# Two attention edits: GpSimd scales the probabilities; ScalarE and VectorE take turns at copying their transposes

## The chip, the cores and the metric

The kernel runs on one core of a Trainium2 chip. The metric is the device time of one execution in microseconds (us); the times are medians over executions. The engines are TensorE (PE, its weight loads PEld), VectorE (DVE), ScalarE (ACT), GpSimd (POOL) and SyncE (SP, which mostly issues transfers). Each engine works through its own instructions in program order.

## The reference

A trunk of two layers over 1024 tokens of width 1024, in f32. Layer 0 mixes with a state-space and a convolution branch and isn't touched by the change. Layer 1 mixes with two attentions, 8 heads each. Every layer ends with a normalised residual and a gated projection.

```python
def masked_softmax(s, mask):
    s = jnp.where(mask, s.astype(jnp.float32), NEG)
    m = jnp.max(s, axis=-1, keepdims=True)
    e = jnp.exp(s - m) * mask
    return e / jnp.maximum(jnp.sum(e, axis=-1, keepdims=True), 1e-30)
...
    # NSA: compressed, selected (top 8 blocks of 64 keys) and windowed (512 keys) attention
    o = g[:, :, 0] * o_cmp + g[:, :, 1] * o_sel + g[:, :, 2] * o_win
...
        # MLA: causal attention over all keys, 64 + 32 features a head
        s = jnp.einsum('bqhd,bkhd->bhqk', qb, k).astype(f32) * scale
        mask = kpos[None] <= (t0 + jnp.arange(Q_BLOCK))[:, None]
        return jnp.einsum('bhqk,bkhd->bqhd', masked_softmax(s, mask), v)
```

## The kernel before

A scheduler that simulates a timeline of the engines orders the instructions of the whole program: the code gives the work and its dependences, and the order on each engine follows from the durations that the scheduler assumes. So an edit that moves an instruction to another engine changes the order on all of them from there on.

**NSA** (`nsa`, about 970 to 1217 us of the profiled execution) takes 8 blocks of 128 queries in the order 1, 2, 0, 3, 4, 5, 6, 7. A block i is done in two halves of 4 heads (`gp`). A half begins with the compressed part (L1315) and then takes two branches: the window (`br=1`, at most 640 keys) and the selection (`br=0`, 128(i+1) keys). **MLA** (`mla`, about 1228 to 1425 us) takes 16 steps: twice the same 8 blocks, 4 heads each, all causal keys.

In both, the 4 heads of a half go through in *groups* of `hg` heads, so many that a group's scores fit one pair of banks: 4 heads up to 256 keys, 2 up to 512, else 1 (`group_size`). A group's way is:

- scores S on TensorE (L1333 and L1338 in NSA; L1518, L1521 and L1522 in MLA; masks L1263) into one of two score buffers in PSUM (`bank2`);
- `softmax_group`: the row maximum, negated, on VectorE (L1234); exp with row sums on ScalarE (L1237), from the score buffer into a probability buffer P in SBUF (which frees the score buffer); the reciprocal of the sum, with the branch's gate, on VectorE (L1241 to L1244); the scaling of P by it, one instruction a head, in place (L1246);
- `transpose_group`: TensorE transposes P in tiles of 128x128 (L1258) into banks of 512 columns, of which three rotate (`ps_t`), and each filled bank is copied to PT in SBUF (L1259). When all the transposes have read P, the buffer is free for another group's exp.

When a branch's four heads are transposed, a run of value matmuls (PV; L1353 in NSA, L1530 in MLA) adds PT times V into the output o, and `store_y` gates and stores it (L1273).

NSA has four probability buffers, MLA three:

```python
                        P = Ps[:, np_ % 4].rearrange("p (h n) -> p h n", h=hg)   # nsa
...
                P = self.t4(name="P").rearrange("p (h n) -> p h n", h=hg)        # mla, 3 buffers
```

GpSimd meanwhile copies gates for groups of 4 heads (L1345), issues the transfers of the query masks (L1295), holds back the load of MLA's rotary keys (L104, `qmslot`) until its place is free, and computes low parts of weights (L108).

Of the kernel before, what the change touches and what calls it, by code (L numbers as in the profile page):

```python
# [11 lines left out]
OP = mybir.AluOpType  # L12
# [10 lines left out]
class Trunk:  # L23
# [1205 lines left out]
    def softmax_group(self, S, n, ginv, P):  # L1229

        nc = self.nc
        hg = S.shape[1]
        nm = self.small.tile([128, 4], F32, tag="nm", name="nm", bufs=4)
        nc.vector.tensor_reduce(out=nm[:, 0:hg], in_=S[:, :, 0:n], op=OP.max, axis=AX.X, negate=True)  # L1234
        sm = self.small.tile([128, 4], F32, tag="sm", name="sm", bufs=4)
        for h in range(hg):
            nc.scalar.activation(out=P[:, h, 0:n], in_=S[:, h, 0:n], func=AF.Exp, bias=nm[:, h:h + 1],  # L1237
                                 accum_out=sm[:, h:h + 1])
        r = self.small.tile([128, 4], F32, tag="sr", name="sr", bufs=4)
        if ginv is None:  # L1240
            nc.vector.tensor_scalar(out=r[:, 0:hg], in0=sm[:, 0:hg], scalar1=1e-30, scalar2=None, op0=OP.max)  # L1241
        else:
            nc.vector.scalar_tensor_tensor(out=r[:, 0:hg], in0=sm[:, 0:hg], scalar=1e-30, in1=ginv, op0=OP.max, op1=OP.mult)
        nc.vector.reciprocal(r[:, 0:hg], r[:, 0:hg])  # L1244
        for h in range(hg):
            nc.vector.tensor_scalar(out=P[:, h, 0:n], in0=P[:, h, 0:n], scalar1=r[:, h:h + 1], scalar2=None, op0=OP.mult)  # L1246

    def transpose_group(self, P, hg, nk, PT, s0):

        nc = self.nc  # L1250
        kb = 4 // hg
        for k0 in range(0, nk, kb):
            n = min(kb, nk - k0)
            ps = self.bank()
            for k in range(n):
                for h in range(hg):
                    c = 128 * (k * hg + h)
                    nc.tensor.transpose(ps[:, c:c + 128], P[:, h, 128 * (k0 + k):128 * (k0 + k) + 128], self.ident)  # L1258
            nc.scalar.copy(PT[:, k0:k0 + n, s0:s0 + hg],  # L1259
                           ps[:, 0:128 * n * hg].rearrange("p (k h t) -> p k h t", h=hg, t=128))  # L1260

    def add_mask(self, S, mask):
        self.nc.tensor.matmul(S, self.ident_bf, mask, start=False, stop=False, skip_group_check=True)  # L1263
# [377 lines left out]
```

## Time and profile before

| | |
|---|---|
| median of 3 runs | 1639.42 us (1637.12 to 1641.62) |
| profiled execution | 1643.63 us, its span 1641.8 us |
| granted TensorE clock, mean | 0.955 of full speed |
| TensorE busy | 93% of the span |
| VectorE, ScalarE, GpSimd busy | 61%, 39%, 22% |

Busy shares are of the whole span, in which NSA and MLA are some 27%. A granted clock of 1.00 is TensorE's upper level, 2.4 GHz, and 0.50 its lower, 1.2 GHz. In the timeline and in grouped rows a matmul's duration overlaps the next one's start; in the chain the pieces adjoin.

### The profile page before, as it was taken

What the parts mean: (1) busy time and instruction counts of PE and PEld (TensorE: products, weight loads), DVE (VectorE), ACT (ScalarE), POOL (GpSimd) and SP (SyncE); (2) the same over time, 40 slices, a digit from 0 to 9 for tenths busy, and PEclk for the clock granted to TensorE, in tenths of its full rate; (3) what the DMA queues carried; (4) which work ended last, traced back from release to release, by engine and by line L of the source; (5) the groups of instructions that cost most, each with busy time, mean ns of one, the idle gap of its engine ahead of it and who ended that gap; (6) DMA issues with size and microseconds to landing.
All of it is one profiled execution on the core that took longest, in us unless ns stands there. A gap on an engine that the chain in (4) does not pass through costs nothing.

```text
span 1641.8 us, 22311 instructions
## 1 busy us (share of the span) xinstructions
PE 1522.7 (93%) x8284; PEld 1193.1 (73%) x8284; DVE 1004.4 (61%) x2248; ACT 636.3 (39%) x1297; POOL 360.4 (22%) x319
## 2 busy tenths in 40 slices
PE   4799899779998999799998979999999999999998
PEld 4697787667786888698876756666666676777787
DVE  6899999778435554751586246777744566444411
ACT  5332122166213333322342127777654565412210
POOL 4528633421225002312222200000000000132400
PEclk8899999889999999899999979999996999999999
DMA  8012453413424324242722264120043230422421
GB/s 244 14 52 79 139 180 111 146 52 129 157 78 142 128 87 135 82 143 85 180 90 90 77 193 125 54 67 22 27 98 85 66 92 25 143 95 94 151 87 68
DMA packets 140380, 168.65 MB, mean 103 GB/s; under 512 B 19432, under 2 KB 107232, under 8 KB 140272
## 3 DMA queue, kind: packets, MB, share of 16 engines
q1 hardware_dynamic: 135568, 155.82, 30.8%
q0 software_dynamic: 4544, 11.38, 2.3%
q8 instruction: 66, 1.08, 0.3%
q14 instruction: 42, 0.34, 0.1%
q10 hardware_dynamic: 160, 0.01, 0.0%
HBM read 112.10 MB, written 50.99 MB: 99 GB/s over the span
## 4 chain that ended last, share of the span: by engine, by line
PE 72%; DVE 17%; DMA 3%; ACT 2%; issue 2%; SPq 2%; POOL 1%; ACTq 0%; DVEq 0%; POOLq 0%
PE S L114 39%; PE tr L1258 7%; DVE conv L264 5%; PE o L1353 5%; PE tr L114 3%; PE o L1530 3%; PE S L1338 2%; PE S L1521 2%; PE S L1522 2%; PE S L1333 2%; PE S L1518 1%; PE tr L802 1%; PE S L1263 1%; SPq L1294 1%; PE tr L973 1%
## 5 line engine op out<-in xcount | busy, mean ns | idle before, releaser
L114 PE MATMUL S<-xT,wt 128*128 128x512 f32 x768 | 188.3, 401 | 4.3 <-DVE ext L249 4.3
L1234 DVE TENSOR_REDUCE nm<-S 128x1 f32<-128x640 f32 (+7 forms) x132 | 129.4, 981 | 101.8 <-PE S L1522 65.1
L114 PE MATMUL S<-X,wt 128*128 128x512 f32 x768 | 184.6, 396 | 5.8 <-ACT wt L107 2.3
L114 PE MATMUL S<-wo,Y 128*128 128x512 f32 x768 | 181.4, 395 | 5.0 <-DVE gb L688 3.6
L114 PE MATMUL S<-wg,hT 128*128 128x512 f32 x720 | 176.8, 403 | 9.5 <-ACT wg L107 4.0
L114 PEld LDWEIGHTS S<-xT,wt 128*128 128x128 f32 x768 | 144.9, 192 | 35.8 <-DVE ext L249 5.1
L114 PEld LDWEIGHTS S<-X,wt 128*128 128x128 f32 x768 | 143.1, 190 | 37.0 <-issue 4.0
L114 PEld LDWEIGHTS S<-wo,Y 128*128 128x128 f32 x768 | 143.8, 189 | 35.7 <-DVE gb L688 3.9
L114 PEld LDWEIGHTS S<-wg,hT 128*128 128x128 f32 x720 | 136.7, 193 | 42.2 <-ACT wg L107 7.3
L264 DVE SCALAR_TENSOR_TENSOR conv<-ext,conv 128x1024 f32<-128x1024 f32 x116 | 148.9, 1284 | 2.3
L108 POOL TENSOR_TENSOR wt<-raw,wt 128x1024 fp32r<-128x1024 f32 x34 | 82.8, 2451 | 115.9 <-ACT wt L107 115.8
L1237 ACT ACTIVATE pslot<-S,nm 128x640 f32<-128x640 f32 (+7 forms) x128 | 89.9, 709 | 25.6 <-DVE nm L1234 14.6
L1259 ACT COPY PT<-tr 128x512 f32<-128x512 f32 (+3 forms) x172 | 80.2, 492 | 46.5 <-PE tr L1258 42.3
L1258 PE MATMUL tr<-ident,pslot 128*128 128x128 f32 x528 | 84.7, 284 | 0.0
L1353 PE MATMUL o<-PT,vslot 128*64 128x256 f32 x528 | 84.5, 391 | 0.0
L1258 PEld LDWEIGHTS tr<-ident,pslot 128*128 128x128 f32 x528 | 58.7, 142 | 29.8 <-issue 20.8
L97 DVE TENSOR_SCALAR rs_v<-ss 128x1 f32<-128x1 f32 x32 | 4.9, 153 | 119.4 <-ACT lh L93 99.1
L1338 PE MATMUL S<-kst,qslot 112*128 112x512 f32 (+3 forms) x192 | 74.4, 400 | 0.0
L1333 PE MATMUL S<-kst,qslot 128*128 128x512 f32 (+3 forms) x192 | 70.3, 366 | 2.3 <-ACT pslot L1237 1.4
L787 POOL TENSOR_TENSOR lh<-lh 128x1024 f32<-128x1024 f32 x16 | 39.9, 2496 | 120.1 <-DVE lh L786 96.5
L852 DVE SCALAR_TENSOR_TENSOR ov<-ov,S 128x1024 f32<-128x1024 f32 (+1 forms) x17 | 19.7, 1157 | 73.3 <-issue 44.7
L93 ACT ACTIVATE lh<-S 128x1024 f32<-128x1024 f32 x16 | 16.4, 1028 | 123.3 <-issue 94.8
(433 smaller groups left out, 2858.8 us busy)
## 6 DMA issues: line engine op xcount, KB each, us to landing
h_dram<-lh POOLq DMA_DIRECT2D x16, 512.0 KB, 3.2
hr<-h_dram SPq DMA_DIRECT2D x14, 512.0 KB, 3.4
raw<-ev_w_in SPq DMA_DIRECT2D x16, 256.0 KB, 4.3
raw<-ev_w_in SPq DMA_DIRECT2D x8, 512.0 KB, 6.9
raw<-ev_w_out SPq DMA_DIRECT2D x8, 512.0 KB, 4.4
t<-ple_gate SPq DMA_DIRECT2D x8, 512.0 KB, 5.9
raw<-ple_gate SPq DMA_DIRECT2D x8, 512.0 KB, 6.3
lh<-x SPq DMA_DIRECT2D x8, 512.0 KB, 3.9
```

The costliest lines, as they stand in the source:

```text
L108: (eng or self.nc.gpsimd).tensor_tensor(lo, raw, hi, OP.subtract)
L114: self.nc.tensor.matmul(ps, l, r, start=n == 0, stop=n == len(seq) - 1)
L264: nc.vector.scalar_tensor_tensor(out=last if s == 30 else acc, in0=src, scalar=wc, in1=acc, op0=OP.mult, op1=OP.add)
L787: nc.gpsimd.tensor_tensor(hv, hv, xr, OP.add)
L1234: nc.vector.tensor_reduce(out=nm[:, 0:hg], in_=S[:, :, 0:n], op=OP.max, axis=AX.X, negate=True)
L1237: nc.scalar.activation(out=P[:, h, 0:n], in_=S[:, h, 0:n], func=AF.Exp, bias=nm[:, h:h + 1], accum_out=sm[:, h:h + 1])
L1258: nc.tensor.transpose(ps[:, c:c + 128], P[:, h, 128 * (k0 + k):128 * (k0 + k) + 128], self.ident)
L1259: nc.scalar.copy(PT[:, k0:k0 + n, s0:s0 + hg], ps[:, 0:128 * n * hg].rearrange("p (k h t) -> p k h t", h=hg, t=128))
L1333: nc.tensor.matmul(o_, QA[:, hd], KA[:, y, ks], start=True, stop=False)
L1338: nc.tensor.matmul(o_, qb[:, hd], KB[:, y, ks], start=False, stop=True)
L1353: nc.tensor.matmul(o[64 * y:64 * y + 64].rearrange("p g t -> p (g t)"), self.vsw[:, k0 + kt, 128 * br + 64 * y:128 * br + 64 * y + 64], PT ...
L1530: nc.tensor.matmul(o[64 * b:64 * b + 64, q], vm[:, kt, vs], PT[:, kt, 2 * b + q], start=(kt == 0), stop=(kt == nk - 1))
```

## The change

The scaling of P goes from VectorE to GpSimd (192 instructions: 128 in NSA, 64 in MLA). The copies of the transposes (258), all on ScalarE before, alternate between ScalarE and VectorE by the number of the bank and of the group.

```diff
         for h in range(hg):
-            nc.vector.tensor_scalar(out=P[:, h, 0:n], in0=P[:, h, 0:n], scalar1=r[:, h:h + 1], scalar2=None, op0=OP.mult)
+            nc.gpsimd.tensor_scalar(out=P[:, h, 0:n], in0=P[:, h, 0:n], scalar1=r[:, h:h + 1], scalar2=None, op0=OP.mult)
 
     def transpose_group(self, P, hg, nk, PT, s0):
...
                     nc.tensor.transpose(ps[:, c:c + 128], P[:, h, 128 * (k0 + k):128 * (k0 + k) + 128], self.ident)
-            nc.scalar.copy(PT[:, k0:k0 + n, s0:s0 + hg],
-                           ps[:, 0:128 * n * hg].rearrange("p (k h t) -> p k h t", h=hg, t=128))
+            copy = nc.vector.tensor_copy if (k0 // kb + s0 // hg) % 2 else nc.scalar.copy
+            copy(PT[:, k0:k0 + n, s0:s0 + hg], ps[:, 0:128 * n * hg].rearrange("p (k h t) -> p k h t", h=hg, t=128))
```

Since the scheduler orders anew, three places are shown in the order of the instructions. In the names, `pslot` is NSA's probability buffers, `tr` a transpose bank, `S` a score buffer, `o` the output, `PT` the transposed probabilities. NSA's groups are numbered in order of the program, 0 to 87; those of block 6 are 56 to 71.

First TensorE in the second half of block 6, from the transposes of group 62 (seven, of a selection head) on. Before, the value matmuls and the transposes of group 63 come next, and then the scores of group 66:

```order
L1258 MATMUL tr<-ident,pslot 128x128 x7
L1353 MATMUL o<-PT,vslot 64x256
L1258 MATMUL tr<-ident,pslot 128x128 x4
L1333 MATMUL S<-kst,qslot 128x512
L1263 LDWEIGHTS mbf
L1263 MATMUL S<-mbf 128x128
L1338 MATMUL S<-kst,qslot 128x512
```

In the changed kernel the same transposes, the first row, are followed at once by the scores of group 68 (selection, 896 keys, in two parts of 512 and 384), then by the transposes of group 63 and the scores of group 69:

```order
L1258 MATMUL tr<-ident,pslot 128x128 x7
L1333 MATMUL S<-kst,qslot 128x512
L1338 MATMUL S<-kst,qslot 128x512
L1333 MATMUL S<-kst,qslot 128x384
L1263 LDWEIGHTS mbf
L1263 MATMUL S<-mbf 128x128
L1338 MATMUL S<-kst,qslot 128x384
L1258 MATMUL tr<-ident,pslot 128x128 x7
L1333 MATMUL S<-kst,qslot 128x512
```

What moved: scores stand six groups ahead of the transposes instead of four.

Second ScalarE at the same place in the changed kernel: two exps of 640 keys (groups 64 and 65), two copies (of groups 61 and 62), the exps of groups 66 and 67, and so on:

```order
L1237 ACTIVATE pslot,sm<-S,nm 128x640 x2
L1260 COPY PT<-tr 128x3x128
L1260 COPY PT<-tr 128x4x128
L1237 ACTIVATE pslot,sm<-S,nm 128x640 x2
L1260 COPY PT<-tr 128x3x128
L1260 COPY PT<-tr 128x4x128
L107 CAST Y_9420<-yt 128x2x128
L1237 ACTIVATE pslot,sm<-S,nm 128x896
```

The exp of group 66 stands behind the copy of group 62; the other copies of these groups are on VectorE.

Third GpSimd at the end of NSA, where it had only the gating copies before; the difference shows the scalings that go in, and those of MLA behind the copy that holds back MLA's keys:

```order
 L104 COPY Y_9420<-Y_9420 128x1 x2
+L1246 TENSOR_SCALAR pslot<-pslot,sr 128x896 x4
+L1246 TENSOR_SCALAR pslot<-pslot,sr 128x640 x4
+L1246 TENSOR_SCALAR pslot<-pslot,sr 128x1024 x4
+L1246 TENSOR_SCALAR pslot<-pslot,sr 128x640 x4
+L1246 TENSOR_SCALAR pslot<-pslot,sr 128x1024 x4
 L104 COPY qmslot<-KAm 96x1
+L1246 TENSOR_SCALAR P<-P,sr 128x128 x4
```

GpSimd's own other work keeps its order, with scalings between.

## Rows read from the trace of the kernel before

**Rows 1.** The page: span, and busy time of each engine with its share.
```profile
span 1641.8 us, 22311 instructions
PE 1522.7 (93%) x8284; PEld 1193.1 (73%) x8284; DVE 1004.4 (61%) x2248; ACT 636.3 (39%) x1297; POOL 360.4 (22%) x319
```
**Rows 2.** Windows: length; busy PE, PEld, DVE, ACT, POOL (instructions); granted clock, DMA share, GB/s.
```profile
1127.00:1168.00 41.00, 41.00 (x282) 27.52 (x281) 29.88 (x69) 28.27 (x65) 0.56 (x2) 1.00 0.12 31
...
1217.00:1228.00 11.00, 6.94 (x54) 4.87 (x52) 1.18 (x3) 3.27 (x10) 0.18 (x1) 0.98 1.03 244
1228.00:1262.00 34.00, 34.00 (x115) 22.15 (x116) 11.64 (x30) 12.17 (x40) 0.00 (x0) 0.51 0.32 85
1262.00:1425.00 163.00, 163.00 (x1163) 113.95 (x1161) 94.48 (x202) 93.64 (x208) 8.03 (x6) 1.00 0.28 79
```
**Rows 3.** The chain that ended last, 1143 to 1152 us: start, duration, what.
```profile
1144.05 1.88 PE o L1353 x16
...
1146.40 0.58 PE o L1353 x2
1146.98 0.42 PE S L1333
...
1148.81 0.23 PE S L1333
...
1149.65 0.79 PE tr L1258 x7
```
**Rows 4.** Waits from 976 to 1430 us: total, times, longest.
```profile
PEld tr L1258 <- issue: 27.3, 88, 0.4
...
PEld tr L1258 <- ACT PT L1259: 5.8, 15, 0.4
```
**Rows 5.** VectorE by line and shape, 960 to 1430 us: busy, mean ns, idle before.
```profile
L1246 DVE TENSOR_SCALAR pslot<-pslot,sr 128x640 f32<-128x640 f32 x40 | 22.1, 553 | 1.3
...
L1273 DVE SCALAR_TENSOR_TENSOR yt<-o,sgpc 128x256 f32<-128x256 f32 x16 | 6.8, 424 | 13.8 <-PE o L1353 13.7
...
L1246 DVE TENSOR_SCALAR pslot<-pslot,sr 128x256 f32<-128x256 f32 x16 | 4.6, 349 | 0.1
...
L1234 DVE TENSOR_REDUCE nm<-S 128x4 f32<-128x512 f32 x6 | 4.1, 692 | 13.3 <-PE S L1522 11.0 <-PE S L1338 2.2
```
**Rows 6.** Windows of line 1246 alone, NSA.
```profile
970.50:1217.00 246.50, 59.70 (x128) 0.99 0.24 65
```
**Rows 7.** GpSimd by line and shape, whole span: busy, mean ns, idle before.
```profile
L1066 POOL TENSOR_SCALAR ginv<-eg 128x24 f32<-128x24 f32 x8 | 2.4, 296 | 38.3 <-ACT eg L1065 38.3
...
L1409 POOL TENSOR_SCALAR rtab<-sink 128x256 f32<-128x256 f32 x2 | 1.7, 850 | 12.0 <-PE tr L1209 7.5 <-PE tr L1413 4.5
...
L1345 POOL COPY gv<-ginv 128x4 f32<-128x4 f32 x8 | 1.4, 188 | 59.6 <-DVE sr L1243 59.6
...
L1410 POOL COPY rtab<-sink 128x256 f32<-128x256 f32 x2 | 0.8, 400 | 0.0
```
**Rows 8.** TensorE's timeline, start of NSA and block 6: start, duration, [idle before, releaser].
```profile
975.96 0.58 PE L1333 MATMUL S<-kst,qslot 128*128 128x256 f32 x1 [1.36 <-ACT pslot L1237]
...
1147.86 0.95 PE L1258 MATMUL tr<-ident,pslot 128*128 128x128 f32 x7
1148.56 0.47 PE L1333 MATMUL S<-kst,qslot 128*128 128x512 f32 x1
```
**Rows 9.** ScalarE's timeline at the same two places.
```profile
975.34 0.48 ACT L1237 ACTIVATE pslot<-S,nm 128x256 f32<-128x256 f32 x1
...
1148.52 0.97 ACT L1259 COPY PT<-tr 128x512 f32<-128x512 f32 x2 [1.60 <-PE tr L1258]
1149.37 0.81 ACT L1237 ACTIVATE pslot<-S,nm 128x640 f32<-128x640 f32 x1
```
**Rows 10.** Windows at the start of NSA, columns as in rows 2.
```profile
975.00:980.00 5.00, 4.04 (x18) 3.67 (x19) 3.31 (x8) 2.83 (x12) 0.19 (x1) 0.50 0.91 236
```
**Rows 11.** TensorE's timeline, first scores of MLA.
```profile
1227.83 0.44 PE L1518 MATMUL S<-KAm,qmslot 128*128 128x128 f32 x1 [4.06 <-DMA qmslot<-qm_dram]
```

## The prediction

> **What bounds the kernel now.** I read the page first, then the busy time of each engine by stage, the chain that ended last inside the attention, the waits there, and single rows where a hop had to be priced. On the page TensorE is busy 93% of the 1641.8 us span, VectorE 61%, ScalarE 39%, GpSimd 22% [rows 1]. By stage it is plainer: in the NSA steps after the first stretch, and in MLA from 1262 us on, TensorE is busy in every slice of its own time (41.00 of 41.0 us, 163.00 of 163 us), while VectorE works 58 to 73% of it and GpSimd almost not at all [rows 2]. The chain agrees: nothing but PE rows, one beginning where the last ended, score matmuls (S), transposes (tr) and value matmuls (o) in turn [rows 3]. So VectorE's and ScalarE's work is hidden, and relieving either is worth nothing as such. Time can change in three ways: TensorE gets other work, TensorE waits where it doesn't now, or the granted clock moves.
>
> From the chain I take TensorE's own prices [rows 3]. A score group of one head at 640 keys lasts from 1148.81 to 1149.65, 0.84 us; its seven transposes 0.79. A run of value matmuls (PV) takes 0.58 us for 2 and 1.88 for 16, so 0.093 each over a fixed 0.39; and the score matmul behind it takes 0.42 instead of 0.23. Each entry into and exit from a PV run therefore costs about 0.39 + 0.15 = 0.54 us.
>
> **What the change moves.** VectorE loses 192 scalings, 59.7 us of its NSA time [rows 6], and gains about half of the 258 copies. Nearest rows for such a copy on VectorE: 424 ns where it reads 256 elements from PSUM, 692 ns where it reads 512 [rows 5], against about 0.5 us each for two on ScalarE [rows 9]. Neither load comes near TensorE's; the cover that hides them is the 41.0 of 41.0 us of PE work, and I cost them at nothing.
>
> GpSimd gets the 192 scalings. The same form has not run there at this width. From above: its tensor_scalar takes 850 ns at 256 elements and 296 at 24, so 2.39 ns an element over 0.24 us. From below: its plain copy takes 400 ns at 256 and 188 at 4, so 0.84 ns an element over 0.185 us [rows 7]. At 640 elements that is 1.77 or 0.72 us, against 0.553 on VectorE [rows 5]. I take the upper, since it is the same operation. NSA has 128 scalings of 67,584 elements a partition in all: 81 to 192 us of GpSimd time in 246.5 us [rows 6]; GpSimd would become NSA's bound only above (246.5 - 30.6)/67,584 = 3.2 ns an element. So it keeps up in throughput, and what it adds is latency, 1.2 us a head.
>
> The Trainium skill, "GPSIMD Engine Reference", section 4.1 (Engine selection), has GpSimd about two times slower than VectorE with two inputs and roughly at line rate with one. The tensor_scalar row speaks against the second half: 850 ns against VectorE's 349 for 256 elements. By the rule a scaling would lie near my lower bound and the sum below would be about 1 us less.
>
> The latency is where the order matters. Because the scheduler counts it, it puts scores farther ahead of transposes: four to five groups in NSA instead of two to three, three to four in MLA instead of one to two. That is the most that four probability buffers and two score banks allow, and it closes a loop: the transposes of group g free the buffer into which the exp of group g+4 writes; that exp frees the score bank which group g+6 needs. I counted, over the order of each kernel, what stands on TensorE between the transposes of g and the scores of g+6. Before, no place in 82 has less than two blocks there. After, 12 places have nothing (the excerpt shows one: seven transposes, then at once the scores that wait on them), 8 have only one block of transposes, 8 only one PV run, one a single score group.
>
> Price of a bare link: the transposes drain for 0.25 us after the next matmul has gone in (1147.86 + 0.95 against 1148.56) [rows 8]; then the exp, 0.81 us [rows 9]; then the hop from its end (975.34 + 0.48) to the waiting matmul at 975.96, 0.14 us [rows 8, 9]. Together 1.2 us in which TensorE, today never idle here, stands still. Of a link with a block between, the block's length is covered.
>
> The sum:
> - 12 bare links at 1.2: +14.4
> - 8 with 0.79 us of transposes between: 8 x 0.4 = +3.2
> - 8 with a PV run between, about 0.9 us: 8 x 0.3 = +2.4
> - one with 0.84 us of scores: +0.4
> - NSA has 80 exits from PV runs instead of 90: -10 x 0.54 = -5.4
> - start of NSA: nothing is there yet to cover the first group's four scalings of 256, 4 x 0.85 instead of 4 x 0.35 us; +2.0 by the upper price, +0.2 by the lower; I take +1.3
> - MLA: 4 short links in 39 places, exits 39 instead of 40: +1.0
>
> That is +17.3 us. On the profiled execution (1643.6 us, its span of 1641.8 and 1.8 around it) it gives 1661; the median of the runs is 4.2 us lower, and from it the same sum gives **1657 us**. Bounds: if half of each bare link is hidden because the exp had been waiting for other reasons and the rest is covered, 7.2 - 5.4 + 0.2 = +2. If a copy of 0.5 us stands ahead of the exp on ScalarE in every link (in the excerpt two do), links cost 1.7, and if the shorter PV count gives nothing: 20.4 + 7.3 + 6.4 + 0.9 + 2.0 + 2.0 = +39. So 1641 to 1678 for this case alone.
>
> **Rivals.** *No change (within 0.3%, 4.9 us, about what a measurement of this kernel can tell).* In the program's order a link looks bare, but TensorE may reach it late: if ScalarE's exps run ahead of the PE queue, the waits shrink. For it: ScalarE is busy only 28.27 of 41.0 us [rows 2]. Against it: the buffer isn't free before the transposes have ended, so no exp can run ahead of that. Links at half price and exits saved give +2: 1641 us.
>
> *Faster.* TensorE's weight loads for transposes wait 27.3 us with no releaser shown ("issue", 88 times) and 5.8 us on ScalarE's copies (15 times), mostly 0.3 to 0.4 us each [rows 4]. If all of these were waits for a transpose bank that ScalarE empties late, two engines that empty in turn would remove up to 33 us, and the sum would be 17 - 33 = -16: 1623 us. It decides where more than half of the "issue" time is bank waits (33 - 17 = 16). Against it: three banks rotate, the exit price of 0.39 appears at each change from value matmuls to transposes whether a copy is pending or not, and only 15 of 103 rows name the copy.
>
> *Much slower.* The waits bring the clock down. At the start of NSA, TensorE waited 1.36 us for an exp [rows 8], and the stretch from 975 to 980 us ran at a granted 0.50, the lower level of 1.2 GHz, though TensorE was busy for 4.04 of the 5 us [rows 10]; the handover to MLA, with a wait of 4.06 us [rows 11] and only 6.94 busy us in 11, was followed by 34 us at 0.51 [rows 2]. Twelve bare links in 246.5 us are one in about 20 us. If a tenth of NSA's TensorE work that now runs at full clock ran at half of it, some 20 us (0.1 x 200) would be added to the 17: 1677 us; a fifth, 1697. GpSimd above 3.2 ns an element would give about as much. Against it: each new wait stands alone, with stretches around it in which TensorE is busy throughout, while the handover, the longer of the two falls, came after 4 us in one piece.
> The Trainium skill, "TensorE: Matmul & The Clock Gate", section "A second HAM failure mode: psum-queue depth-cycling", says that frequent small idles between groups of matmuls, as banks are cycled, can make the clock go back and forth. That is this rival; the rows above show two falls after waits, and the later NSA stretch without waits at 1.00.
>
> **How the numbers follow.** Main case 0.52, no change 0.16, faster 0.17, much slower 0.15. The predicted time is the main case's, 1657. The main case lies above +0.3% nearly throughout, so faster 0.17, same 0.16, slower 0.67. The range from 1632 to 1680 leaves out about half of each outer case, some 0.17 together.
>
> **What would show it.** Right: in the stretches between 1046 and 1217 us TensorE is no longer busy throughout but idles some 10 to 20 us in all, in pieces of about a microsecond in front of score matmuls (L1333), released by the exp (L1237), each right behind transposes; a step like the one from 1127 to 1168 us lasts 43 to 44 us instead of 41.0 [rows 2]; MLA hardly changes; GpSimd's scalings of 640 take 1.5 to 1.9 us and its busy share of NSA stays below 80%. Wrong: waits in front of transposes released by GpSimd (L1246), which would mean that GpSimd's price or its queue (the scalings stand in it with the mask loads, L1295, and the copy that gates the MLA keys, L104) is the bound; a granted clock under 0.95 in NSA after its first stretch; or transposes whose 0.39 us behind PV runs are gone, which would mean the copies had been on the path all along.

## The result: 76 us slower

The changed kernel takes 1715.59 us (median of 4, 1714.35 to 1721.71) against 1639.24 for the kernel before: ratio 1.0463, 95% interval 1.0438 to 1.0488. The forecast had the sign, and a time 59 us too short, outside its range. The page of the changed kernel, span and busy times, beside [rows 1]:

```profile
span 1714.2 us, 22444 instructions
PE 1539.1 (90%) x8284; PEld 1197.3 (70%) x8284; DVE 990.7 (58%) x2182; ACT 581.5 (34%) x1171; POOL 677.0 (39%) x511
```

Of the 72.4 us between the profiled spans, NSA has 48 and MLA 22; NSA begins 1.8 us later and what follows MLA is as long as before. Windows of NSA and of MLA as a whole, first the kernel before, then the changed one (columns as in [rows 2]):

```profile
970.30:1227.80 257.50, 251.19 (x1691) 166.66 (x1690) 179.22 (x427) 176.68 (x455) 7.94 (x18) 0.99 0.27 72
1227.80:1426.80 199.00, 198.97 (x1292) 137.51 (x1292) 106.71 (x231) 105.82 (x247) 8.03 (x6) 0.92 0.29 82
```
```profile
972.10:1277.90 305.80, 261.04 (x1685) 169.02 (x1683) 172.01 (x383) 140.72 (x369) 211.44 (x146) 0.99 0.23 61
1277.90:1498.80 220.90, 211.41 (x1319) 145.02 (x1320) 100.11 (x209) 87.25 (x207) 119.26 (x70) 0.91 0.27 74
```

The granted clock is what it was: 0.99 in NSA, 0.91 in MLA against 0.92. TensorE is idle for 44.8 us of NSA instead of 6.3. No engine is full: GpSimd is busy 69%. What TensorE's matmuls wait for, in NSA (the row of line 1518 is MLA's first score):

```profile
PE S L1333 <- ACT pslot L1237: 21.2, 25, 1.4
PE o L1353 <- DVE PT L1260: 8.6, 11, 1.3
PE o L1353 <- ACT PT L1260: 5.3, 11, 0.7
PE S L1518 <- DMA qmslot<-qm_dram: 3.3, 1, 3.3
PE tr L1258 <- DVE PT L1260: 1.6, 3, 0.8
```

Two things are to be seen. Scores wait for the exp, as forecast; value matmuls wait for the copies, which was not. And there is no row in which a matmul waits for GpSimd. Weight loads for transposes do, briefly, 0.4 us at most:

```profile
PEld tr L1258 <- POOL pslot L1246: 4.2, 11, 0.4
```

One link of each kind, from the timeline (rows of the loads are left out). Scores behind transposes, twice:

```profile
1142.70 0.84 PE L1258 MATMUL tr<-ident,pslot 128*128 128x128 f32 x6
...
1143.36 0.59 ACT L1260 COPY PT<-tr 128x512 f32<-128x512 f32 x1 [2.24 <-PE tr L1258]
...
1143.85 0.80 ACT L1237 ACTIVATE pslot<-S,nm 128x640 f32<-128x640 f32 x1
...
1144.79 0.51 PE L1333 MATMUL S<-kst,qslot 128*128 128x512 f32 x1 [1.25 <-ACT pslot L1237]
...
1145.74 0.82 PE L1258 MATMUL tr<-ident,pslot 128*128 128x128 f32 x6
...
1146.54 0.79 ACT L1237 ACTIVATE pslot<-S,nm 128x640 f32<-128x640 f32 x1 [1.80 <-issue]
...
1147.48 0.50 PE L1333 MATMUL S<-kst,qslot 128*128 128x512 f32 x1 [0.92 <-ACT pslot L1237]
```

In the first link the transposes end at 1143.54; the exp for which they free a buffer starts at 1143.85, behind a copy on ScalarE, and ends at 1144.65; the scores that need its score buffer start at 1144.79. That is 0.31 + 0.80 + 0.14 = 1.25 us idle. The second has no copy before the exp, and TensorE is idle for 0.92. The prediction's 1.2 counts the transposes' drain of 0.25 in, which lies ahead of this idle time: with it the two links cost about 1.5 and 1.2. Value matmuls behind transposes:

```profile
1110.35 0.74 PE L1258 MATMUL tr<-ident,pslot 128*128 128x128 f32 x5
...
1111.29 0.68 DVE L1260 COPY PT<-tr 128x512 f32<-128x512 f32 x1
...
1112.03 1.30 PE L1353 MATMUL o<-PT,vslot 128*64 128x256 f32 x10 [0.94 <-DVE PT L1260]
```

These read what was transposed a moment ago, so they wait for the copy. To weigh the kinds I took every matmul of NSA from both traces and added up the time from its start to the next one's start by the pair of lines. Transposes then scores grew by 25.9 us, transposes then value matmuls by 12.4, transposes then transposes by 7.0; leaving PV runs fell by 4.5 (to transposes -12.7, to scores +8.2). Together 40.8 of the 48.3.

GpSimd's scalings, by shape, beside [rows 5, 7]:

```profile
L1246 POOL TENSOR_SCALAR pslot<-pslot,sr 128x640 f32<-128x640 f32 x40 | 75.1, 1888 | 30.1 <-DVE sr L1244 28.2 <-ACT PT L1260 1.8
...
L1246 POOL TENSOR_SCALAR pslot<-pslot,sr 128x256 f32<-128x256 f32 x16 | 14.5, 923 | 0.3
```

They take 3.4 and 2.6 times VectorE's 553 and 349 ns. Yet they are mostly early: in blocks 4 to 7 (64 groups) the time from the end of a group's last scaling to its first transpose has a median of 6.2 us, against 3.6 before. So GpSimd doesn't hold TensorE up in person; transposes stand later in TensorE's order than they have to. That became the theory to test. **Theory O:** the scheduler arranges the program as if the scaling took longer than it does, runs scores ahead as far as the buffers allow and puts transposes late; TensorE, in order, then meets bare links. **Theory G:** GpSimd's own time on the chip costs it. **Theory C:** copies on VectorE, queued behind its row maxima, are late. (In the expectations of the first four runs, Theory L is O and G not yet told apart.)

### The profile page after: what moved, and what is told of

The parts are those of the page before. It is cut to its first block, busy times and chain, and to the rows that moved or that the text cites. A ratio compares the mean times of both kernels' runs of the same rounds, so it can differ in the third digit from the quotient of the medians.

```text
span 1714.2 us, 22444 instructions
## 1 busy us (share of the span) xinstructions
PE 1539.1 (90%) x8284; PEld 1197.3 (70%) x8284; DVE 990.7 (58%) x2182; ACT 581.5 (34%) x1171; POOL 677.0 (39%) x511
## 5 line engine op out<-in xcount | busy, mean ns | idle before, releaser
L1246 POOL TENSOR_SCALAR pslot<-pslot,sr 128x640 f32<-128x640 f32 (+7 forms) x128 | 203.9, 1606 | 71.6 <-DVE sr L1244 63.3
L1246 POOL TENSOR_SCALAR P<-P,sr 128x128 f32<-128x128 f32 (+7 forms) x64 | 111.0, 1746 | 97.5 <-DVE sr L1244 75.3
L1333 PE MATMUL S<-kst,qslot 128*128 128x512 f32 (+3 forms) x192 | 72.4, 377 | 23.5 <-ACT pslot L1237 21.2
L1258 PE MATMUL tr<-ident,pslot 128*128 128x128 f32 x528 | 78.9, 280 | 3.1 <-DVE PT L1260 1.6
L1260 ACT COPY PT<-tr 128x512 f32<-128x512 f32 x88 | 43.0, 489 | 92.3 <-PE tr L1258 92.3
```

Source lines behind the costliest of these rows:

```text
L1246: nc.gpsimd.tensor_scalar(out=P[:, h, 0:n], in0=P[:, h, 0:n], scalar1=r[:, h:h + 1], scalar2=None, op0=OP.mult)
L1260: copy(PT[:, k0:k0 + n, s0:s0 + hg], ps[:, 0:128 * n * hg].rearrange("p (k h t) -> p k h t", h=hg, t=128))
L1333: nc.tensor.matmul(o_, QA[:, hd], KA[:, y, ks], start=True, stop=False)
```

## The experiments

Each ran four times beside the kernel before, no_scaling ten times. NSA and MLA are their lengths in the one profiled execution, MLA to the end of its last value matmul; before 257.5 and 199.0, changed 305.8 and 221.2 (the window above ends 0.3 us early).

| run | time us | ratio, 95% interval | NSA | MLA |
|---|---|---|---|---|
| gps_only | 1721.29 | 1.0511 [1.0495, 1.0526] | 305.8 | 220.2 |
| alt_only | 1650.55 | 1.0075 [1.0059, 1.0092] | 255.2 | 198.3 |
| half | 1650.80 | 1.0082 [1.0059, 1.0106] | 256.4 | 200.2 |
| ring | 1716.03 | 1.0478 [1.0456, 1.0501] | 304.1 | 225.8 |
| b_order_a | 1706.31 | 1.0400 [1.0365, 1.0434] | 318.8 | 198.4 |
| a_order_b | 1684.46 | 1.0266 [1.0220, 1.0312] | 272.8 | 221.1 |
| gp_copy | 1702.27 | 1.0383 [1.0350, 1.0416] | 293.3 | 219.9 |
| near | 1695.16 | 1.0338 [1.0309, 1.0368] | 275.1 | 230.9 |
| both_fixed_order | 1673.12 | 1.0189 [1.0152, 1.0226] | 274.1 | 201.7 |
| gps_fixed_order | 1674.81 | 1.0209 [1.0182, 1.0235] | 274.8 | 206.8 |
| alt_fixed_order | 1656.67 | 1.0088 [1.0055, 1.0121] | 264.8 | 201.9 |
| no_scaling | 1648.86 | 1.0047 [1.0031, 1.0063] | 255.7 | 201.7 |

**One edit at a time.** gps_only is the first hunk of the diff, alt_only the second.

> Only the scaling goes to GpSimd; all copies stay on ScalarE. Theory L (the latency of GpSimd's scaling, through the order that it brings about, makes the whole loss): TensorE waits before scores behind transposes and before value matmuls as in the full change, about 21 and 14 us in NSA; 1700 to 1720 us. Theory C (the 14.6 us of waits before value matmuls come from copies that stand late in VectorE's queue): these waits shrink to under 5 us, the waits before scores stay; 1690 to 1703 us.

> Only the copies alternate; VectorE scales. Theory L: nothing waits, scores stand four groups ahead, TensorE stays busy throughout NSA; 1632 to 1645 us. Theory C: value matmuls wait for VectorE's copies, 5 to 15 us in NSA and some in MLA; 1648 to 1665 us. If the waits of TensorE's loads for transposes were waits for banks that ScalarE empties late (the faster rival of the prediction): 1610 to 1632 us.

GpSimd's scaling alone gives the whole loss. It is 6 us slower than both edits, at a lower granted clock: 0.948 to 0.952 over its executions, against 0.954 to 0.960. Alternating copies alone cost 12 us; the profiled execution, the fastest of its four, shows 3 of them, and in it neither NSA nor MLA is longer. That time lies in the range of Theory C, but no value matmul waits for a copy there. TensorE's waits in NSA with GpSimd's scaling alone:

```profile
PE S L1333 <- ACT pslot L1237: 19.9, 26, 1.4
PE o L1353 <- ACT PT L1259: 12.6, 27, 1.0
PE tr L1258 <- ACT PT L1259: 4.6, 6, 1.9
```

The waits before value matmuls are there with every copy on ScalarE, so Theory C falls for this change. The faster rival falls too: with alternating copies TensorE's loads for transposes wait less (21.4 us, 68 times, against 27.3 and 88 in [rows 4]), and NSA is only 2.3 us shorter.

**Half of each scaling on GpSimd.**

```diff
+            m = n // 256 * 128
-            nc.gpsimd.tensor_scalar(out=P[:, h, 0:n], in0=P[:, h, 0:n], scalar1=r[:, h:h + 1], scalar2=None, op0=OP.mult)
+            nc.vector.tensor_scalar(out=P[:, h, m:n], in0=P[:, h, m:n], scalar1=r[:, h:h + 1], scalar2=None, op0=OP.mult)
+            if m:
+                nc.gpsimd.tensor_scalar(out=P[:, h, 0:m], in0=P[:, h, 0:m], scalar1=r[:, h:h + 1], scalar2=None, op0=OP.mult)
```

> The full change, but GpSimd scales only the first half of each row of P (whole tiles of 128) and VectorE the rest, at the same time. Theory L: the latency of a head falls from 1.89 to some 1.0 us at 640 keys, the scheduler goes only four groups ahead, the loop through the probability buffers stays open: a loss of 0 to 15 us, 1639 to 1655 us. Rival (the loss goes with GpSimd's busy time, 204 us in NSA, or with what it shares with VectorE): half the loss, 1670 to 1685 us.

Nothing is lost beyond what alternating copies cost alone, although the scalings are a little slower side by side: VectorE's scalings of 384 take 509 ns here against 416 before, GpSimd's of 256 take 1004 against 923 in the changed kernel. In this order scores stand four groups ahead (63 of 88 times; this count is one higher than the prediction's, by which before has two or three and the changed kernel four or five). The loss doesn't grow in step with GpSimd's work: it sets in between half and all of it, with the order.

**More probability buffers.** A group takes its own width from the same 4096 columns.

```diff
-                        P = Ps[:, np_ % 4].rearrange("p (h n) -> p h n", h=hg)
-                        np_ += 1
+                        if np_ + hg * n > 4096:
+                            np_ = 0
+                        P = Pf[:, np_:np_ + hg * n].rearrange("p (h n) -> p h n", h=hg)
+                        np_ += hg * n
```

> The full change, but NSA's four fixed probability buffers of 1024 become a ring in the same memory in which a group takes only its own width, so that five to six groups fit (six of 640 keys). Theory L, with the loop through four buffers as its cause: the waits before scores behind transposes (19.5 us) fall to under 8, time 1695 to 1706 us. Rival (the scheduler only goes farther ahead, up to seven or eight groups, and closes the same loop one buffer later): waits as before, 1710 to 1722 us.

The rival holds: scores now stand seven or eight groups ahead in half of the places, and the same waits come back (here line 1355 is the value matmuls):

```profile
PE S L1333 <- ACT pslot L1237: 21.8, 32, 1.4
PE o L1355 <- DVE PT L1260: 5.5, 8, 1.2
PE o L1355 <- ACT PT L1260: 4.3, 8, 1.0
```

So the four buffers are where the loop closes, not why.

**Orders exchanged.** TensorE's scores, transposes and value matmuls are chained one behind the other, without any waiting for results, in an order read from the other kernel. The chaining, with the list shortened:

```diff
+PE_ORDER = (
+    "s24t2s8t4s4t4s4t2v4t2s4t3v2t1s4v2t7v2t1v2s4t6v4s4t8v1s4t6v5s4t6v1t4s8v5t2s8t6v1s8t4s8v5t8v1s4t6s4t1v5t3v2t1s4t"
...
+        for k, n in re.findall(r"([stv])(\d+)", PE_ORDER):
+            for _ in range(int(n)):
+                mm = next(queue[k])
+                if last is not None:
+                    self.tc.add_manual_dep(mm.ins, last.ins.name, mybir.DependencyInfo(
+                        mybir.DependencyClass.NoSync, mybir.DependencyReason.DATA), reason="order")
+                last = mm
```

> The engines of before (VectorE scales, ScalarE copies), but NSA's scores, transposes and value matmuls are chained on TensorE in exactly the order that they have in the changed kernel. Theory O (the order that the scheduler makes for a slow GpSimd costs the time, not GpSimd on the chip): NSA lasts 290 to 305 us instead of 257.5, in all 1672 to 1690 us. Theory G (GpSimd's time on the chip costs it): as before, 1636 to 1648 us.

> The engines of the changed kernel (GpSimd scales, copies alternate), but NSA's scores, transposes and value matmuls are chained on TensorE in exactly the order that they have in the kernel before. Theory O: NSA lasts 255 to 265 us, MLA, which is not chained, keeps its 221; in all 1658 to 1672 us. Theory G: NSA stays at 290 us or more, with waits of transposes for the scaling; 1690 to 1715 us.

With the changed kernel's order and not one scaling on GpSimd, NSA takes 318.8 us, longer than in the changed kernel itself; MLA, left alone, is as before. TensorE's waits in that NSA:

```profile
PE S L1355 <- ACT pslot L1247: 30.2, 34, 1.8
PE o L1375 <- ACT PT L1270: 9.3, 19, 1.2
```

The other way round, GpSimd scales in the order of before: NSA takes 272.8 us, and now the rows name GpSimd:

```profile
PE tr L1269 <- POOL pslot L1257: 9.3, 12, 1.7
PE tr L1269 <- ACT PT L1272: 2.2, 2, 1.2
```

Both expectations of Theory O missed in size: the time of b_order_a is 16 us above its range, and a_order_b is 12 us above. Under the short look-ahead Theory G has a share as well: NSA is 15 us longer than before, and 9.3 of them are waits for GpSimd.

**A shorter operation on GpSimd.** The scaling line becomes `nc.gpsimd.tensor_copy(P[:, h, 0:n], P[:, h, 0:n])`.

> The full change, but in place of the scaling GpSimd copies P onto itself (the division by the row sums is left out in both attentions). By the rows of before a copy takes 0.72 us at 640 elements, not 1.9; the order on TensorE goes as far ahead as with the scaling. Theory O: the loss stays, 1700 to 1720 us. Theory G: it falls with GpSimd's time, 1640 to 1675 us.

The order stays as far ahead (five or six groups in 73 of 88 places) and so does most of the loss, 64 of 76 us, though GpSimd needs 0.723 us a head instead of 1.888:

```profile
L1246 POOL COPY pslot<-pslot 128x640 f32<-128x640 f32 x40 | 28.9, 723 | 77.3 <-ACT pslot L1237 77.3
```

**An order of my own for NSA:** the scores of group j chained behind the transposes of group j-4.

```diff
+                                if s_ == c == 0 and len(self.done) >= 4:
+                                    self.tc.add_manual_dep(mm.ins, self.done[-4].ins.name, mybir.DependencyInfo(
+                                        mybir.DependencyClass.NoSync, mybir.DependencyReason.DATA), reason="order")
```

> The full change, but in NSA the scores of group j are chained behind the last transposes of group j-4 on TensorE, so that scores stand at most four groups ahead, in a regular order of its own. Theory O: no bare loop is left; NSA 255 to 270 us, MLA 221, in all 1655 to 1675 us. Theory G: 1690 to 1715 us.

NSA is 31 us shorter than in the changed kernel, but not as short as expected, and MLA is 10 us longer, at a granted clock of 0.87 against 0.91. So the time falls into Theory G's range, but its mechanism isn't there: in NSA matmuls wait 1.2 us for GpSimd. The waits before scores are gone (one of 1.4 us is left). In their place value matmuls wait for VectorE's copies:

```profile
PE o L1358 <- DVE PT L1261: 14.7, 24, 1.9
...
PE S L1335 <- ACT pslot L1238: 1.4, 1, 1.4
```

Here Theory C's mechanism does act, in an order that puts few blocks between a copy and its reader.

**Order of before in NSA and MLA, edits apart and together.**

> The engines of the changed kernel, with scores, transposes and value matmuls chained on TensorE in the order of the kernel before, now in NSA and in MLA. Theory O: NSA 273 us as in the run with NSA's order alone; MLA falls from 221 to 200 to 210; in all 1662 to 1676 us. Rival (in MLA it is GpSimd's time on the chip: an order only one or two groups ahead doesn't cover 2.5 to 3 us a head): MLA 215 us or more, 1678 to 1695 us.

> Only the scaling goes to GpSimd, copies stay on ScalarE; TensorE's order in NSA and MLA is that of the kernel before. If what is left of the loss under a fixed order is GpSimd's scaling alone: as with both edits under that order, within 6 us. If it is the copies that stand late in VectorE's queue: 1640 to 1650 us.

> Only the copies alternate, VectorE scales; TensorE's order in NSA and MLA is that of the kernel before. If the 12 us that the alternating copies cost alone came from the order too: 1633 to 1644 us. If the copies on VectorE cost time in themselves: 1646 to 1656 us.

MLA returns from 221 to 202 us in both_fixed_order, with GpSimd scaling as slowly as in the changed kernel. But that profiled execution was the fastest of its four (1663.5 us, the others 1672 to 1675), and its MLA has a granted clock of 0.95. The fairer pair is gps_only and gps_fixed_order, with 0.91 and 0.92 in MLA: 220.2 against 206.8 us. So some 13 of MLA's 21 us were a loss of order; most of the rest is other work that now stands inside MLA (25.4 us on TensorE in gps_fixed_order, 18.2 before; see the next section). Both edits together and GpSimd's scaling alone agree within 2 us. The alternating copies cost 16 us alone under this order and 12 under their own, with intervals that overlap, and the expectation that the 12 came from the order missed. That the copies cost it in themselves isn't shown: 5 of the 16 us lie before NSA begins, and in NSA matmuls wait 0.6 us for a copy on VectorE. Nor does any run chain the kernel before to its own order; alt_fixed_order bounds what the chaining can cost, copies included, at 16 us.

**VectorE relieved.** The kernel before without the scaling line.

> The kernel before without the scaling (the division by the row sums is left out in both attentions), so that VectorE has 91 us less to do and nobody more; the scheduler orders anew. If VectorE's load is covered by TensorE, as the prediction has it: 1630 to 1644 us. If relieving VectorE were worth something by itself: 1600 to 1628 us.

Missed on the side against the change: with 91 us less on VectorE and nothing more anywhere, the kernel is 8 us slower than before (NSA 1.8 us shorter, MLA 2.7 longer). Relief for VectorE is worth nothing here. Its order is a new one, too: scores stand only two groups ahead (73 of 88 times).

## Why the prediction had the sign and missed the size

- **The bound.** Right. TensorE was the bound, VectorE's relief brought nothing (no_scaling), and half of the scaling on GpSimd cost nothing (half against alt_only).
- **GpSimd's price.** Nearly right: 1.888 us against 1.77 from the upper end at 640 elements; 203.9 us in NSA against 192. It never became NSA's bound. GpSimd's copy took 0.723 us, the lower end. The rule of the Trainium skill, "GPSIMD Engine Reference", section 4.1 (Engine selection), that one-input work runs at roughly line rate there, describes the copy better than the scaling: 0.723 and 1.888 us against VectorE's 0.553 for the scaling.
- **Bare links between transposes and scores.** Right in mechanism, a little small: 20.4 us from 29 places in the sum; the trace has 26 waits of 19.5 us idle, 25.9 from start to start, since after a stop the next matmul no longer overlaps the one before. The 12 links with nothing between are idle for 12.4 us, 15.7 from start to start, where the sum has 14.4; of the 8 with a PV run between only one waits, 0.14 us, where the sum has 2.4. Part of the total was luck: waits in places that the sum left out made up for it.
- **Fewer PV runs.** Near: -5.4 forecast, -4.5 found. The price had a slip: 0.42 - 0.23 is 0.19, not 0.15, which gives -5.8.
- **"I cost them at nothing", of the copies.** The step that failed in NSA. I took the copies' cover, 41.0 of 41.0 us of TensorE work, from the order of before, while my own next step said that the order changes. In the new order value matmuls more often stand right behind transposes that they read (behind the last of their own branch in 10 of 32 branches, before in 4), and there a copy of 0.6 to 0.7 us has no cover: +12.4 us. Between transposes it is +7.0, of which 3.0 are waits for a free bank; the rest goes with 34 more pairs of that kind (an estimate of 4 us, at the 0.12 that a pair took before). I counted the pairs of transposes and scores in the new order and did not count transposes and value matmuls, which stand in the same rows.
- **MLA, "+1.0".** Failed by 21 us. I counted its links and no more. Part of it is work that moved in: matmuls of line 114, most of them the out-projection's, before MLA's end, first the kernel before, then the changed one:

```profile
1227.80:1426.50 198.70, 18.18 (x75) 12.71 (x75) 0.91 0.29 81
```
```profile
1277.90:1498.80 220.90, 26.64 (x104) 19.27 (x104) 0.91 0.27 74
```

  That is 8.5 us more in MLA, and the rest of the program didn't get shorter by it (215.0 us before, 215.1 after). The remainder is 9 us of waits, mostly for exps and copies, and a longer stay at the lower clock level around the handover (32.1 us at 0.50 and then 30 at 0.87, against [rows 2]'s 34.00 at 0.51), which is worth some 3 us, an estimate from these clocks. Under the order of before MLA was 206.8 with GpSimd's scaling alone and the clock of before.
- **The range** ended at +41 because its upper bound stretched the links I had counted and had no term for pairs that I had not.
- **The rivals.** No change and faster: false. Much slower by a falling clock: false as to the cause, NSA kept 0.99, with 26 stops in front of scores, up to 1.4 us idle each, and 22 in front of value matmuls. But such falls do occur. In the changed kernel's MLA a wait of 1.60 us ended at 1327.22, and the granted clock from 1325 to 1335 us was 0.83. In gps_only's NSA waits of 1.91 and 0.63 us came within 3 us, and from 1118 to 1132 us TensorE ran at 0.51:

```profile
1117.34 0.33 PE L1258 MATMUL tr<-ident,pslot 128*128 128x128 f32 x1 [1.91 <-ACT PT L1259]
1118.29 0.80 PE L1333 MATMUL S<-kst,qslot 128*128 128x512 f32 x1 [0.63 <-ACT pslot L1237]
```
```profile
1118.00:1132.00 14.00, 11.83 (x43) 7.45 (x45) 4.25 (x11) 4.75 (x14) 8.01 (x5) 0.51 0.15 37
```

Sorted by the fixed order: of the 76 us some 44 (76 - 33) go when TensorE keeps its order of before in NSA and MLA; some 33 stay with the engines of the change and with the chaining, of which waits of transposes for GpSimd show 9.3 us in NSA. The two shares hold for this way round only: the order of NSA alone, with the engines of before, costs 68 us (b_order_a). That the order alone suffices in NSA is shown by that run. Why the scheduler goes so far ahead is only argued: two groups without a scaling, three or four with VectorE's, four with half of it on GpSimd, five or six with all of it or with a copy of 0.7 us there, as if its duration for GpSimd were long; no run shows what it assumes. Where the alternating copies lose their 12 to 16 us stays open: under their own order neither NSA nor MLA is longer in the profiled execution, and what follows MLA is (220.9 against 215.0 us, with a granted clock of 0.97 against 0.98).

## What to carry to other kernels

Where a scheduler orders the program, an edit that moves an instruction to a slower engine is first of all an edit of every engine's order: count in the new order, for the engine that is the bound, every kind of producer and consumer pair that has come close together, not only the pair that the edit touches. When the engine that was given the work is hardly waited for and the bound engine waits all the same, the loss is in the order, and chaining the bound engine to the old order tells how much of it, up to what the chaining costs. A work's cover must be read in the order that the change makes, not in the trace of before.

## What was not expected of the hardware

At 640 f32 elements a partition GpSimd took 1.888 us for a multiplication by a per-partition factor and 0.723 for a copy in place, a factor of 2.6 for the same bytes. And a stop costs TensorE more than the idle time that the waits show: 19.5 us idle in 26 places went with 25.9 us from start to start. How the clock takes such stops differs: the changed kernel's NSA kept 0.99 through all of them, while in gps_only 1.91 and 0.63 us close together were followed by 14 us at 0.51.
